# Norm gain applied in the turned copies, and other slots for down's first operands, in a two-layer encoder

## The chip, the core and the metric

The kernel runs on one core of a Trainium2 chip. The metric is the device time of one execution, in microseconds (us). The engines are TensorE (PE: matmuls; PEld is its weight load), VectorE (DVE), ScalarE (ACT), GpSimd (POOL) and SyncE (SP, which issues the DMAs). Each engine works through its own instructions in order and waits on semaphores for what others must finish first.

## The reference

Two encoder layers over 512 tokens of 1024 channels. Each layer is a feed-forward, a mixer of four attention groups and a second feed-forward, each followed by a residual sum and a norm:

```
def _layer_norm(x, g, b):
    mu = jnp.mean(x, -1, keepdims=True)
    xc = x - mu
    var = jnp.mean(xc * xc, -1, keepdims=True)
    return xc * lax.rsqrt(var + NORM_EPS) * g + b

def _swiglu(h, w_gu, w_down):
    gate, up = jnp.split(h @ w_gu, 2, axis=-1)
    return (jax.nn.silu(gate) * up) @ w_down

def reference(x, ...):
    alpha = (2 * DEPTH) ** 0.25
    for l in range(DEPTH):
        x = _layer_norm(alpha * x + 0.5 * _swiglu(x, ffn_w_gu[l, 0], ffn_w_down[l, 0]), ln_g[l, 0], ln_b[l, 0])
        mix = _token_mixers(x, w_in[l], ...)
        x = _layer_norm(alpha * x + mix, ln_g[l, 1], ln_b[l, 1])
        x = _layer_norm(alpha * x + 0.5 * _swiglu(x, ffn_w_gu[l, 1], ffn_w_down[l, 1]), ln_g[l, 2], ln_b[l, 2])
    return x
```

The feed-forward's hidden width is 2816.

## The kernel before

**Tiles.** The tokens lie in four tiles x0 to x3 of 128 tokens by 1024 channels. Every matmul operand is split into a high part (a cast, on ScalarE) and a low part (the rest, a subtraction on VectorE), and each product is made of three matmuls: high by high, high by low, low by high.

**The feed-forward** (`ffn`, L322) works through 11 pairs (`Pair`, L370); a pair is 256 columns of gate and of up. Each pair is a two-by-two block product, done with seven smaller products (`product`, L356) of 24 matmuls of 128x256 instead of eight. Their weights are sums of four loaded blocks (`prep_rest`, L392), their x operands are sums of blocks of the turned x, called al1 to al7. Products 1 and 2 go to banks ga and gb (`run12`), and `run_rest` (L420) goes on with 6 in ga, 5 in a new bank gc, then 7 in ga, 3 in gc and 4 in ga. Between 6 and 7 ScalarE copies ga out as u2 (L425), since the partial sum is needed by itself. The weights' high parts wh (L351) and low parts wl (L352) have rings of four buffers each: the cast of the fourth product after one waits until that one has been read.

**Down** (L472 to L511) then multiplies the 22 chunks of 128 hidden columns by w_down, into eight banks acc. A chunk's operands hh (cast, L480) and hl (subtraction, L481) are made from the stored h0 and h1 of its pair, into slots of two tags: even pairs into "v", odd ones into "p" (L476). The "v" slots also hold al3 (L160), which every pair reads.

**The norm** (`layer_norm`, L291) adds acc to x, takes statistics (bn_stats, bn_aggr), computes the factor on GpSimd (L303, L304), and then makes four VectorE operations of 128x512 a tile: subtract the mean and multiply by the gain (L307, two halves), multiply by the factor and add the offset (L314). Where a norm leads into a feed-forward, `to_al` (L186) turns the tile by eight TensorE transposes into two PSUM banks (xtp), copies them out and makes the splits: tiles 0 and 1 give al1 and al2 and the kept copies ac, tiles 2 and 3 give al4, 5, 7, 6 and 3, in this order. This happens four times: at the start of the program, from the mixer of each layer to its second feed-forward, and between the layers.

**What sets the order.** The program is written out in Python; a scheduler then orders each engine's instructions by program order and its own estimate of when they can start. So an instruction written later can stand earlier on its engine.

Of the kernel before, what the change touches and what calls it, by code (L numbers as in the profile page):

```python
# [11 lines left out]
F32 = mybir.dt.float32  # L12
# [60 lines left out]
def tile_encoder(ctx: ExitStack, tc: tile.TileContext, d: dict, out: bass.AP):  # L73
# [111 lines left out]

    def to_al(t):  # L186

        i = t % 2
        if t < 2:
            for g, b in turned_x(t):  # L190
                kept[g, i] = b4("hl", "ac")
                se.copy(kept[g, i], b)
                al_split(1 + g, i, b, -1.0)
            return
        (_, b0), (_, b1) = list(turned_x(t))
        a22 = b4("tb", "a22")
        se.copy(a22, b1)
        al_split(4, i, b1, -1.0)
        t5, t7 = b4("tb", "t5"), b4("tb", "t7")
        ve.tensor_tensor(t5, b0, a22, op=ALU.subtract)  # L200
# [90 lines left out]
    def layer_norm(t, accs, c, gb, shared=False):  # L291


        stt = sm.tile([P, 2, 6], F32, tag="bn", name="bn", bufs=2)
        xs = [x[t][:, n * FD:(n + 1) * FD] for n in range(2)]
        for n in range(2):
            ve.scalar_tensor_tensor(xs[n], accs[n], c * INV_A, xs[n], op0=ALU.mult, op1=ALU.add)
        for n in range(2):
            ve.bn_stats(stt[:, n], xs[n])
        mv = sm.tile([P, 2], F32, tag="mv", name="mv", bufs=2)  # L300
        ve.bn_aggr(mv, stt)  # L301
        rs = sm.tile([P, 2], F32, tag="rs", name="rs", bufs=2)
        ge.tensor_scalar(rs[:, 0:1], mv[:, 1:2], 1.0, EPS * INV_A * INV_A, op0=ALU.mult, op1=ALU.add)  # L303
        ge.tensor_tensor(rs[:, 1:2], rs[:, 0:1], mhalf[:, 0:1], op=ALU.pow)  # L304
        both = range(1 if shared else 2)
        for n in both:
            ve.scalar_tensor_tensor(xs[n], xs[n], mv[:, 0:1], gb[2 * n], op0=ALU.subtract, op1=ALU.mult)  # L307
        if shared:
            ge.tensor_scalar(rs[:, 0:1], mv[:, 0:1], rs[:, 1:2], -1.0, op0=ALU.mult, op1=ALU.mult)
            se.activation(xs[1], xs[1], AF.Identity, bias=rs[:, 0:1], scale=rs[:, 1:2])  # L310
            ge.tensor_tensor(xs[1], xs[1], gb[2], op=ALU.mult)
            ge.tensor_tensor(xs[1], xs[1], gb[3], op=ALU.add)
        for n in both:
            ve.scalar_tensor_tensor(xs[n], xs[n], rs[:, 1:2], gb[2 * n + 1], op0=ALU.mult, op1=ALU.add)  # L314


# [5 lines left out]
    def ffn(l, f, last, to_next):  # L322
# [47 lines left out]
        class Pair:  # L370
# [21 lines left out]
            def prep_rest(self):  # L392
                r = self.r
                add = lambda o, a, b: ve.tensor_tensor(o, a, b, op=ALU.add)  # L394
                add(r[11], r[11], r[12])
                t2 = raw_tile("t2")
                add(t2, r[11], r[22])
                self.w[6] = parts4(t2)
                self.w[5] = parts4(r[11])
                add(r[12], r[12], r[22])  # L400
                self.w[7] = parts4(r[12])
                self.w[3] = parts4(r[22])
                add(r[21], r[21], t2)
                self.w[4] = parts4(r[21])
                return self
# [14 lines left out]
            def run_rest(self):  # L420
                v3 = lambda t: t.rearrange("p (c t) -> p c t", c=2)
                a = self.a
                product(6, a, self.w[6], False)
                u2 = v3(tmp("u2"))
                se.copy(u2, a)  # L425
# [30 lines left out]
        p1.run12()  # L456
        gb = gain_tiles(l, 2 * f)
        if opening:
# [5 lines left out]
        for j in range(2, NB):  # L464
            p = Pair(j).load().prep12().prep_rest()
            p.run12()
            p.run_rest()
        acc = [[bank(tag, f"acc{t}{n}") for n, tag in enumerate(two)]
               for t, two in enumerate((("pt", "pt"), ("pv", "pj"), ("pj", "pj"), ("s", "s")))]
        hparts = {}  # L470

        def h_of(c, t):  # L472

            j = c // 2
            if j not in hparts:
                tag = ("v", "p")[j % 2] if c < NC - TAIL else "oT"  # L476
                hparts[j] = []
# [21 lines left out]
        if to_next:  # L499
            to_next[0]()  # L500
        for t in range(NT):
            for n in range(2):
                for i in range(TAIL):
                    down(t, NC - TAIL + i, ws[i], (n,))
            layer_norm(t, acc[t], 0.5, gb, last and t == NT - 2)
            if last:
# [155 lines left out]
    def mixer(l):  # L662
# [796 lines left out]
        def finish(t, accs):  # L1459
            layer_norm(t, accs, 1.0, lngb)  # L1460
            to_al(t)

# [17 lines left out]
    for l in range(DEPTH):  # L1480
        ffn(l, 0, False, (new_xT, to_xT))
        mixer(l)
        ffn(l, 1, l == DEPTH - 1, (new_al, to_al) if l < DEPTH - 1 else None)

# [21 lines left out]
```

## Time and profile before

| | us |
|---|---|
| median of 3 runs | 1984.5 (1984.44 to 1985.53) |
| profiled execution | 1989.4 |
| its span in the trace | 1987.6 |
| mean granted TensorE clock in it | 0.983 of full |
| start of the program, 0 to 50: PE busy | 36.48 of 50 |
| pairs of the first feed-forward, 50 to 250: PE, DVE, ACT busy | 198.07, 157.55, 101.14 of 200 |
| first down, 250 to 310: PE, DVE busy | 60.00, 24.84 of 60 |
| first mixer, 310 to 590: PE, DVE busy | 268.84, 206.42 of 280 |
| its transition into the next feed-forward, 632 to 680: PE, DVE busy | 34.76, 46.22 of 48 |

The span is cut by time: the start, then in each layer pairs, down, mixer, transition, pairs, down. In the profile's lines a group reads "line engine operation output<-input form", with the buffers' numbers left out; a bracket holds the idle time before an instruction and what released it. Matmuls are pipelined, so the distance from one start to the next is the time one takes, and the duration shown is longer.

### The profile page before, as it was taken

The numbers are of one execution on the slowest core, as the hardware profiler recorded it, in microseconds if no ns is written. First come the engines' busy times: TensorE is split into PE (matmuls) and PEld (weight loads), VectorE is DVE, ScalarE is ACT, GpSimd is POOL, SyncE is SP. The second block draws the span as 40 slices with busy tenths as digits, with TensorE's granted clock in tenths as the row PEclk, the third lists the DMA queues.
The fourth block names the chain that finished last, engine by engine and source line by source line (L and its number), as shares of the span: only waits on it lengthen the run. The fifth ranks groups of instructions, "written<-read, shape, count | busy, mean of one in ns | idle before, by whom it ended". The sixth has DMA issues, their size and how long they took to land.

```text
span 1987.6 us, 31884 instructions
## 1 busy us (share of the span) xinstructions
PE 1906.2 (96%) x12396; PEld 1735.7 (87%) x12396; DVE 1450.0 (73%) x2229; ACT 960.0 (48%) x1593; POOL 269.5 (14%) x411
## 2 busy tenths in 40 slices
PE   7999999999999899999999999999999979999998
PEld 6999988788887899988889999887887869999886
DVE  7887742858999978763598787337689998878535
ACT  5544532248774554443155545322587745444421
POOL 0000000335741000000000000004366300000001
PEclk9999999999999899999999999999999989999999
DMA  5323233343442333332223323331533424232321
GB/s 196 120 88 115 97 101 105 86 112 89 112 112 86 96 110 103 107 127 96 85 77 106 121 92 99 110 120 47 141 93 92 118 74 128 92 112 84 106 97 62
DMA packets 156487, 204.53 MB, mean 103 GB/s; under 512 B 14064, under 2 KB 122608, under 8 KB 156336
## 3 DMA queue, kind: packets, MB, share of 16 engines
q1 hardware_dynamic: 156336, 202.49, 33.7%
q8 instruction: 98, 1.61, 0.3%
q14 instruction: 53, 0.43, 0.1%
HBM read 177.42 MB, written 2.10 MB: 90 GB/s over the span
## 4 chain that ended last, share of the span: by engine, by line
PE 85%; DVE 8%; POOL 2%; ACT 2%; issue 2%; DMA 1%; SPq 0%; DVEq 0%; POOLq 0%; ACTq 0%
PE ga L249 25%; PE acc L249 23%; PE gc L249 13%; PE gb L249 6%; PE nat L249 5%; PE op L249 3%; PE sc L249 3%; PE pjt L249 2%; PE pv L249 2%; PE ptb L109 2%; DVE p L591 1%; PE xtp L109 1%; DVE al L178 1%; POOL wl L222 0%; DVE x L314 0%
## 5 line engine op out<-in xcount | busy, mean ns | idle before, releaser
L249 PE MATMUL ga<-al,wh 128*128 128x256 f32 x2752 | 392.5, 285 | 12.4 <-ACT wh L351 11.7
L351 ACT CAST wh<-b 128x1024 fp32r<-128x1024 f32 x256 | 267.7, 1049 | 280.2 <-issue 164.7
L352 DVE TENSOR_TENSOR wl<-b,wh 128x1024 fp32r<-128x1024 f32 x256 | 311.2, 1219 | 120.9 <-ACT wh L351 120.9
L249 PEld LDWEIGHTS ga<-al,wh 128*128 128x128 f32 x2752 | 360.2, 194 | 13.0 <-ACT wh L351 12.1
L222 DVE TENSOR_TENSOR wl<-wr,wh 128x1024 fp32r<-128x1024 f32 (+1 forms) x92 | 112.2, 1220 | 232.1 <-ACT wh L221 232.1
L249 PE MATMUL acc<-wh,hh 128*128 128x512 f32 x704 | 272.9, 390 | 6.7 <-ACT hh L480 6.7
L249 PE MATMUL acc<-wh,hl 128*128 128x512 f32 x704 | 276.6, 393 | 1.1 <-DVE hl L481 1.1
L249 PE MATMUL acc<-wl,hh 128*128 128x512 f32 x704 | 276.5, 393 | 0.2 <-DVE wl L222 0.2
L221 ACT CAST wh<-wr 128x1024 fp32r<-128x1024 f32 (+2 forms) x98 | 101.5, 1040 | 269.1 <-PE acc L249 226.0
L249 PE MATMUL ga<-al,wl 128*128 128x256 f32 x1376 | 224.3, 286 | 0.0
L303 POOL TENSOR_SCALAR rs<-mv 128x1 f32<-128x1 f32 x24 | 9.9, 412 | 1498.8 <-DVE mv L301 1498.7
L249 PE MATMUL gc<-al,wh 128*128 128x256 f32 x1408 | 201.1, 285 | 4.6 <-ACT al L177 4.3
L249 PEld LDWEIGHTS ga<-al,wl 128*128 128x128 f32 x1376 | 192.2, 194 | 0.6 <-DVE wl L352 0.3
L249 PEld LDWEIGHTS gc<-al,wh 128*128 128x128 f32 x1408 | 184.3, 194 | 5.2 <-ACT al L177 4.5
L249 PEld LDWEIGHTS acc<-wh,hh 128*128 128x128 f32 x704 | 132.1, 188 | 34.5 <-ACT hh L480 7.5
L249 PEld LDWEIGHTS acc<-wh,hl 128*128 128x128 f32 x704 | 133.3, 189 | 30.3 <-DVE hl L481 2.8
L249 PEld LDWEIGHTS acc<-wl,hh 128*128 128x128 f32 x704 | 133.1, 189 | 28.4 <-DVE wl L222 0.6
L249 PE MATMUL gc<-al,wl 128*128 128x256 f32 x704 | 113.6, 284 | 0.0
L394 DVE TENSOR_TENSOR b<-b,b 128x1024 f32<-128x1024 f32 x88 | 107.4, 1220 | 5.5 <-DMA b<-in_ffn_w_gu_dram 4.2
L249 PEld LDWEIGHTS gc<-al,wl 128*128 128x128 f32 x704 | 97.6, 193 | 0.0
L351 ACT CAST wh<-t 128x1024 fp32r<-128x1024 f32 x44 | 46.2, 1049 | 105.6 <-DVE t L394 105.6
L249 PE MATMUL gb<-al,wh 128*128 128x256 f32 x640 | 90.8, 285 | 0.0
(280 smaller groups left out, 3414.6 us busy)
## 6 DMA issues: line engine op xcount, KB each, us to landing
b<-in_ffn_w_gu_dram SPq DMA_DIRECT2D x176, 512.0 KB, 3.6
wr<-in_ffn_w_down_dram SPq DMA_DIRECT2D x88, 512.0 KB, 3.2
wr<-in_w_in_dram SPq DMA_DIRECT2D x30, 512.0 KB, 3.7
k<-ph SPq DMA_DIRECT2D x64, 128.0 KB, 2.4
wr<-in_w_out_dram SPq DMA_DIRECT2D x16, 512.0 KB, 3.6
qs<-ph SPq DMA_DIRECT2D x32, 128.0 KB, 2.4
ln_g<-in_ln_g_dram SPq DMA_DIRECT2D x12, 256.0 KB, 4.1
ln_b<-in_ln_b_dram SPq DMA_DIRECT2D x12, 256.0 KB, 4.7
```

The costliest lines, as they stand in the source:

```text
L109: te.transpose(o, a, ident)
L178: ve.tensor_tensor(l[:, :, cs], v, h[:, :, cs].bitcast(F32), op=ALU.subtract)
L221: se.copy(h[:, w], r[:, w])
L222: (lo or ve).tensor_tensor(l[:, q], r[:, q], h[:, q].bitcast(F32), op=ALU.subtract)
L249: te.matmul(o, a, b, start=start, stop=stop, **kw)
L303: ge.tensor_scalar(rs[:, 0:1], mv[:, 1:2], 1.0, EPS * INV_A * INV_A, op0=ALU.mult, op1=ALU.add)
L351: se.copy(h, r[:, q])
L352: ve.tensor_tensor(lo, r[:, q], h.bitcast(F32), op=ALU.subtract)
L394: add = lambda o, a, b: ve.tensor_tensor(o, a, b, op=ALU.add)
L591: ve.tensor_tensor_reduce(p, sb, nd, -h.slope, h.sink[0] if h.sink else 3.0e38, ALU.add, ALU.min, m)
```

## The change

The norms that lead into a feed-forward go through a new `norm_to_al`. It leaves gain and offset out of x: ScalarE normalises the tile with mean and factor alone (two activations of 128x512 with scale and bias, and GpSimd makes the bias in a third small operation). The turned copy gets gain and offset while ScalarE copies it out of PSUM, in `whole`: there a channel is a partition, so each of the eight blocks of 128x128 is one activation with a column of scale and a column of bias from `gt`, a small tile loaded from a new input `ln_t` that the host lays out. The splits then read the copy, not PSUM. x itself is needed with its gain only at the residual sum after down, so `gain_later` makes it up by four VectorE operations a tile, written after pairs 2 to 5. In `to_al` the splits of tiles 2 and 3 come in the order 5, 6, 7, 4, 3, also at the start of the program, where there is no gain. In the pairs product 5 now stands before product 6, and its weights are made first. The norm's gain tiles are loaded at pair 6 instead of at the start of the feed-forward. For down, the tags of the operands are swapped: even pairs into "p", odd ones into "v".

```diff
-    def to_al(t):
+    def to_al(t, gt=None):
+        def whole(g, b, tag, name):
+            o = b4(tag, name)
+            if gt is None:
+                se.copy(o, b)
+                return o, b
+            for k in range(4):
+                kk = 4 * g + k
+                se.activation(o[:, k], b[:, k], AF.Identity, bias=gt[:, 1, kk:kk + 1], scale=gt[:, 0, kk:kk + 1])
+            return o, o
...
-                kept[g, i] = b4("hl", "ac")
-                se.copy(kept[g, i], b)
+                kept[g, i], b = whole(g, b, "hl", "ac")
                 al_split(1 + g, i, b, -1.0)
...
-        a22 = b4("tb", "a22")
-        se.copy(a22, b1)
-        al_split(4, i, b1, -1.0)
+        a22, b1 = whole(*turned[1], "tb", "a22")
...
         ve.tensor_tensor(t5, b0, a22, op=ALU.subtract)
+        al_split(5, i, t5)
         ve.tensor_tensor(t7, b0, kept[0, i], op=ALU.subtract)
-        al_split(5, i, t5)
         t6 = kept[0, i]
         ve.tensor_tensor(t6, t6, t5, op=ALU.subtract)
+        al_split(6, i, t6)
         al_split(7, i, t7)
-        al_split(6, i, t6)
+        al_split(4, i, b1, -1.0)
...
+    def norm_to_al(t, accs, c, l, i, gb):
+
+        if t == 0:
+            gt = sm.tile([P, 2, 8], F32, tag="gt", name="gt", bufs=1)
+            load(gt, d["ln_t"][l, i])
+            gained[:] = [gt, gb]
...
+        rs, mv = norm_factors(stt)
+        ge.tensor_scalar(rs[:, 0:1], mv[:, 0:1], rs[:, 1:2], -1.0, op0=ALU.mult, op1=ALU.mult)
+        for n in range(2):
+            se.activation(xs[n], xs[n], AF.Identity, bias=rs[:, 0:1], scale=rs[:, 1:2])
+        to_al(t, gained[0])
+
+    def gain_later(t):
+        for n in range(2):
+            xs = x[t][:, n * FD:(n + 1) * FD]
+            ve.tensor_tensor(xs, xs, gained[1][2 * n], op=ALU.mult)
+            ve.tensor_tensor(xs, xs, gained[1][2 * n + 1], op=ALU.add)
...
                 add(r[11], r[11], r[12])
+                self.w[5] = parts4(r[11])
                 t2 = raw_tile("t2")
                 add(t2, r[11], r[22])
                 self.w[6] = parts4(t2)
-                self.w[5] = parts4(r[11])
...
-                product(6, a, self.w[6], False)
-                u2 = v3(tmp("u2"))
-                se.copy(u2, a)
                 c = self.bank("pj", "gc")
                 product(5, c, self.w[5], True)
                 p5 = v3(tmp("p5"))
                 se.copy(p5, c)
+                product(6, a, self.w[6], False)
+                u2 = v3(tmp("u2"))
+                se.copy(u2, a)
                 product(7, a, self.w[7], False)
...
-        gb = gain_tiles(l, 2 * f)
...
+            if gained and j < 6:
+                gain_later(j - 2)
+            if j == 6:
+                gained.clear()
+                gb = gain_tiles(l, 2 * f)
...
-                tag = ("v", "p")[j % 2] if c < NC - TAIL else "oT"
+                tag = ("p", "v")[j % 2] if c < NC - TAIL else "oT"
```

What the scheduler makes of it is shown at three places. The rows are an engine's instructions in order (line, operation, output<-input with the buffers' numbers, shape, and the engines waited for).

The first place is VectorE in the first transition, where the norm's third and fourth tiles meet the splits. Before, x3's statistics end at bn_6961, and its aggregate, gain and offset follow the splits of x2:

```order
L299 BN_STATS bn_6961<-x3_89 128x6 [waits DVE_49]
L200 TENSOR_TENSOR t5_6923<-xtp_6909,a22_6919 128x512 [waits Activation_49]
L181 SCALAR_TENSOR_TENSOR al4_6761<-xtp_6914,al4_6761 128x4x128 [waits PE_49,Activation_49]
...
L178 TENSOR_TENSOR al3_6774<-ac_6825,al3_6773 128x2x128 [waits Activation_49]
L301 BN_AGGR mv_6966<-bn_6961 128x2
L418 TENSOR_TENSOR s1_7054<-gb_7056,s1_7054 128x512 [waits PE_49]
L178 TENSOR_TENSOR al3_6776<-ac_6825,al3_6775 128x2x128 [waits Activation_49]
L307 SCALAR_TENSOR_TENSOR x3_89<-x3_89,mv_6966,ln_g_6753 128x512 [waits DVE_49]
L307 SCALAR_TENSOR_TENSOR x3_89<-x3_89,mv_6966,ln_g_6757 128x512
L314 SCALAR_TENSOR_TENSOR x3_89<-x3_89,rs_6968,ln_b_6755 128x512 [waits DVE_49,Pool_49]
L314 SCALAR_TENSOR_TENSOR x3_89<-x3_89,rs_6968,ln_b_6759 128x512 [waits DVE_49]
```

Now the same place reads so (mv_6984 is x3's aggregate, t5_6940 the first split of x2):

```order
L348 BN_STATS bn_6979<-x3_89 128x6 [waits DVE_49]
L439 TENSOR_TENSOR b21_7031<-b21_7031,t2_7176 128x1024
L330 BN_AGGR mv_6984<-bn_6979 128x2 [waits DVE_49,Pool_49]
L358 TENSOR_TENSOR x0_86<-x0_86,ln_g_6753 128x512
L397 TENSOR_TENSOR wl_7111<-b11_7106,wh_7110 128x1024 [waits DMAHW7_49,Activation_49]
L359 TENSOR_TENSOR x0_86<-x0_86,ln_b_6755 128x512 [waits DVE_49]
L358 TENSOR_TENSOR x0_86<-x0_86,ln_g_6757 128x512
L215 TENSOR_TENSOR t5_6940<-t7_6935,a22_6930 128x512 [waits Activation_49]
...
L178 TENSOR_TENSOR al3_6774<-ac_6829,al3_6773 128x2x128 [waits Activation_49]
L397 TENSOR_TENSOR wl_7115<-b21_7108,wh_7114 128x1024 [waits DMAHW6_49]
```

x3's aggregate and pair 0's last sum (b21) moved ahead of x2's splits, five rows of later gain moved in (three of x0's are shown), and wl_7115, the low weights of pair 1's product 2, stand behind the splits.

The second place is TensorE in a pair of the first feed-forward; 40 other pairs read alike (in three, six matmuls stand where ten do here). Before, product 6 (al6) is followed by all of product 5 (al5):

```order
L249 MATMUL ga_730<-al6_92,wl_709 128x256 x4
L249 MATMUL gc_809<-al5_91,wh_712 128x256 x8
L249 MATMUL gc_809<-al5_91,wl_713 128x256 [waits DVE_49]
L249 MATMUL gc_809<-al5_91,wl_713 128x256 x3
L249 MATMUL gc_809<-al5_91,wh_712 128x256 x8
L249 MATMUL gc_809<-al5_91,wl_713 128x256 x4
```

Now ten matmuls of product 3 (al3) follow it, and then product 7 (al7), which waits for ScalarE:

```order
L265 MATMUL ga_722<-al6_92,wl_705 128x256 x4
L265 MATMUL gc_775<-al3_102,wh_713 128x256 [waits Activation_49]
...
L265 MATMUL gc_775<-al3_105,wh_713 128x256
L265 MATMUL gc_775<-al3_102,wl_714 128x256 [waits DVE_49]
L265 MATMUL gc_775<-al3_102,wl_714 128x256
L265 MATMUL ga_722<-al7_93,wh_709 128x256 [waits Activation_49]
```

In the same pair ScalarE now reads as follows; before, u2's copy stood behind the cast for product 4, and p5's behind that for the next pair's product 1:

```order
L396 CAST wh_718<-b21_683 128x1024 [waits PE_49,Activation_49]
L471 COPY p5_800<-gc_775 128x512 [waits PE_49]
L396 CAST wh_917<-b11_909 128x1024 [waits DMAHW3_49,PE_49,Activation_49]
L474 COPY u2_826<-ga_722 128x512 [waits PE_49]
L396 CAST wh_921<-b21_911 128x1024 [waits DMAHW4_49,PE_49,Activation_49]
```

In this order wh_917 belongs to product 1 of the next pair and takes the buffer of product 6's weights; u2's copy stands behind it.

The third place is ScalarE around the first down. Before, the operands of chunk 0 (hh_2755) are cast behind the last pair's s2:

```order
L221 CAST wh_2857<-wr_2855 128x1024 [waits DMAHW5_49,DVE_49,PE_49]
L441 ACTIVATE s2_2737<-ga_2554 128x512 [waits DVE_49,PE_49]
L480 CAST hh_2755<-h0_520 128x512
L480 CAST hh_2759<-h1_524 128x512
L480 CAST hh_2891<-h0_911 128x512
```

Now they stand in the second pair, at row 51 of the engine instead of 172:

```order
L486 ACTIVATE s2_514<-ga_176 128x512 [waits DVE_49,PE_49]
L529 CAST hh_2755<-h0_512 128x512 [waits DVE_49]
L396 CAST wh_543<-b21_293 128x1024 [waits DVE_49,PE_49,Activation_49]
L471 COPY p5_572<-gc_547 128x512 [waits PE_49]
L529 CAST hh_2759<-h1_516 128x512 [waits DVE_49]
```

and behind the last s2 it is the second pair's operands that are cast first (hh_2823 and hh_2827, chunks 2 and 3):

```order
L486 ACTIVATE s2_2737<-ga_2554 128x512 [waits DVE_49,PE_49]
L529 CAST hh_2823<-h0_675 128x512
L529 CAST hh_2827<-h1_679 128x512
L529 CAST hh_2959<-h0_1131 128x512
L529 CAST hh_3403<-h0_2735 128x512 [waits DVE_49]
```

Chunk 0's operands moved from the end of the pairs to their beginning, and the second pair's took their place.

More of the change, by code (lines that the diff above doesn't have):

```diff
@@ L299, in layer_norm @@
             ve.bn_stats(stt[:, n], xs[n])
[L300 to L304, printed above, removed]
+        rs, mv = norm_factors(stt)
         both = range(1 if shared else 2)
@@ L314, in layer_norm, with norm_factors @@
             ve.scalar_tensor_tensor(xs[n], xs[n], rs[:, 1:2], gb[2 * n + 1], op0=ALU.mult, op1=ALU.add)
+    def norm_factors(stt):
+        mv = sm.tile([P, 2], F32, tag="mv", name="mv", bufs=2)
+        ve.bn_aggr(mv, stt)
+        rs = sm.tile([P, 2], F32, tag="rs", name="rs", bufs=2)
+        ge.tensor_scalar(rs[:, 0:1], mv[:, 1:2], 1.0, EPS * INV_A * INV_A, op0=ALU.mult, op1=ALU.add)
+        ge.tensor_tensor(rs[:, 1:2], rs[:, 0:1], mhalf[:, 0:1], op=ALU.pow)
+        return rs, mv
+    gained = []
+    def norm_to_al(t, accs, c, l, i, gb):
[3 more added lines that the diff above has]
+            gained[:] = [gt, gb]
+        stt = sm.tile([P, 2, 6], F32, tag="bn", name="bn", bufs=2)
+        xs = [x[t][:, n * FD:(n + 1) * FD] for n in range(2)]
+        for n in range(2):
+            ve.scalar_tensor_tensor(xs[n], accs[n], c * INV_A, xs[n], op0=ALU.mult, op1=ALU.add)
+            ve.bn_stats(stt[:, n], xs[n])
+        rs, mv = norm_factors(stt)
+        ge.tensor_scalar(rs[:, 0:1], mv[:, 0:1], rs[:, 1:2], -1.0, op0=ALU.mult, op1=ALU.mult)
[3 more added lines that the diff above has]
+    def gain_later(t):
+        for n in range(2):
+            xs = x[t][:, n * FD:(n + 1) * FD]
+            ve.tensor_tensor(xs, xs, gained[1][2 * n], op=ALU.mult)
+            ve.tensor_tensor(xs, xs, gained[1][2 * n + 1], op=ALU.add)
     TAIL = 4
@@ L499, in ffn @@
         if to_next:
-            to_next[0]()
+            (to_next[0] if len(to_next) > 1 else new_al)()
         for t in range(NT):
@@ L504, in ffn @@
                     down(t, NC - TAIL + i, ws[i], (n,))
+            if to_next and len(to_next) == 1:
+                to_next[0](t, acc[t], 0.5, l, 2 * f, gb)
+                continue
             layer_norm(t, acc[t], 0.5, gb, last and t == NT - 2)
@@ L1459, in finish @@
         def finish(t, accs):
-            layer_norm(t, accs, 1.0, lngb)
-            to_al(t)
+            norm_to_al(t, accs, 1.0, l, 1, lngb)
         for gns, ts in (("B", range(NA)), ("AB", range(NA, NT))):
@@ L1482, in tile_encoder @@
         mixer(l)
-        ffn(l, 1, l == DEPTH - 1, (new_al, to_al) if l < DEPTH - 1 else None)
+        ffn(l, 1, l == DEPTH - 1, (norm_to_al,) if l < DEPTH - 1 else None)
 _INS = ["x", "w_in", "win_sink", "mla_q_norm", "mla_w_uq", "mla_kv_norm", "mla_w_ukv", "ax_q_norm", "ax_k_norm",
@@ L1497 @@
     given.update(shape_constants())
+    rows = [given[n].reshape(DEPTH, 3, KD, P).transpose(0, 1, 3, 2) for n in ("ln_g", "ln_b")]
+    given["ln_t"] = np.ascontiguousarray(np.stack(rows, 3))
     for n, a in given.items():
```

9 lines of the change are left out of this document (7 added, 2 removed).

## The prediction

> **What bounds the kernel now.** I read the page first, for the busy shares and the chain of work that ended last. Then I read the list of TensorE's waits, and last the timeline at the places that it names.
>
> ```profile
> span 1987.6 us, 31884 instructions
> PE 1906.2 (96%) x12396; PEld 1735.7 (87%) x12396; DVE 1450.0 (73%) x2229; ACT 960.0 (48%) x1593; POOL 269.5 (14%) x411
> PE 85%; DVE 8%; POOL 2%; ACT 2%; issue 2%; DMA 1%; SPq 0%; DVEq 0%; POOLq 0%; ACTq 0%
> ```
>
> TensorE is busy for 96% of the span, and 85% of the chain is its own. An edit can therefore win only where TensorE waits or runs below full clock, and it loses wherever it makes a new wait. The waits (engine, tile and line, then who released it and the line; total us, times, longest) that the edits touch are these:
>
> ```profile
> PE xtp L109 <- DVE x L314: 21.4, 8, 6.5
> PE ga L249 <- ACT wh L351: 11.7, 2, 6.0
> PE acc L249 <- ACT hh L480: 6.7, 4, 1.7
> ```
>
> The next rows are windows: the stretch, its length, then busy time of PE, PEld, DVE, ACT and POOL, and the granted clock. The first two hold the transitions from a mixer to a feed-forward (I call them T1 and T3), the third the one from feed-forward to feed-forward (T2), the fourth one pair of the steady loop, the last the entry into a down projection.
>
> ```profile
> 590.00:680.00 90.00, 76.76 (x486) 69.24 (x485) 86.83 (x144) 46.16 (x84) 9.79 (x17) 0.92 0.28 86
> 1570.00:1662.00 92.00, 79.12 (x487) 71.63 (x486) 87.56 (x143) 46.05 (x83) 9.77 (x17) 0.91 0.27 85
> 1000.00:1035.00 35.00, 31.24 (x234) 30.16 (x233) 34.30 (x49) 18.40 (x29) 2.72 (x4) 0.90 0.26 76
> 1078.13:1098.29 20.16, 20.16 (x170) 20.16 (x169) 16.45 (x17) 10.44 (x14) 0.00 (x0) 1.00 0.34 105
> 245.50:252.80 7.30, 5.37 (x17) 3.88 (x16) 5.26 (x9) 5.18 (x8) 0.00 (x0) 0.77 0.47 153
> ```
>
> In T1 and T3 TensorE idles for about 13 us, and VectorE is busy for 96% of the time: there VectorE is the bound. In the steady pair TensorE never stops, and VectorE has 3.7 us to spare.
>
> **Down's first operands.** This term is the surest. Timeline of TensorE at the first entry (start, duration; the bracket is the idle time before it and its releaser):
>
> ```profile
> 245.01 0.64 PE L249 MATMUL ga<-al,wl 128*128 128x256 f32 x4
> 247.31 1.20 PE L249 MATMUL acc<-wh,hh 128*128 128x512 f32 x4 [1.66 <-ACT hh L480]
> 248.77 0.50 PE L249 MATMUL acc<-wh,hl 128*128 128x512 f32 x1 [0.27 <-DVE hl L481]
> ...
> 252.75 0.40 PE L249 MATMUL acc<-wl,hh 128*128 128x512 f32 x1
> 252.99 0.39 PE L249 MATMUL acc<-wh,hh 128*128 128x512 f32 x1
> 253.22 0.39 PE L249 MATMUL acc<-wh,hl 128*128 128x512 f32 x1
> ```
>
> The four matmuls at 245.01 (0.12 each) are issued by 245.49. Then 14 go out up to 252.75, in 5.44 us from the first; at full clock, 0.23 each as in the last rows, they would be out by 245.49 + 3.22 = 248.71. So an entry loses 4.04 us: 1.93 of idle time and 2.11 of slow clock behind it. In the new order (shown above) the casts and subtractions for chunk 0 stand in the second pair, some 200 us ahead, and the first accumulating matmul waits for nothing. Those of the next two chunks stay behind the last pair, but they are wanted 48 x 0.23 = 11.0 us in, and the same operations of before let matmuls go 2 and 3.5 us in. Four entries: **-16.2**. The bounds are -7.7, if only the idle time goes, and -16.2.
>
> By the Trainium skill ("TensorE: Matmul & The Clock Gate", "What's actually happening") the clock falls only after a whole idle window of about 3.4 us. By that rule these gaps would not slow the matmuls, and the edit would be worth its idle time alone. The trace disagrees: 1.66 us idle are followed by 14 matmuls in 5.44 us, at a granted clock of 0.77.
>
> **Product 7's wait (new).** Here the change loses. One steady pair, TensorE and then ScalarE:
>
> ```profile
> 1077.65 0.64 PE L249 MATMUL ga<-al,wl 128*128 128x256 f32 x4
> 1078.13 1.12 PE L249 MATMUL gc<-al,wh 128*128 128x256 f32 x8
> 1081.01 1.12 PE L249 MATMUL ga<-al,wh 128*128 128x256 f32 x8
> 1077.91 1.05 ACT L351 CAST wh<-b 128x1024 fp32r<-128x1024 f32 x1 [1.02 <-PE ga L249]
> 1078.86 0.58 ACT L425 COPY u<-ga 128x512 f32<-128x512 f32 x1
> ```
>
> Product 6 ends in bank ga; u2 is copied out behind a cast of 1.05 us that the same product released, and is done at 1079.44, or 1.31 us after TensorE went on. Product 7 writes the same bank. Before, the 24 matmuls of product 5 lie between (2.88 us, 0.12 each), and the copy has 1.57 us to spare. Now product 5 is ahead, and in 41 of 44 pairs ten matmuls of product 3 lie between: 1.20 us. ScalarE has the same pair of rows in the new order, since a cast again reuses product 6's slot. So product 7 misses the bank by 0.11, and I add 0.05 for the release. Starting again costs too:
>
> ```profile
> 633.15 0.38 PE L249 MATMUL ga<-al,we 128*128 128x256 f32 x1 [0.42 <-DVE bn L299]
> 633.37 0.28 PE L249 MATMUL ga<-al,wh 128*128 128x256 f32 x1
> 1021.52 1.10 PE L249 MATMUL ga<-al,wh 128*128 128x256 f32 x7 [0.68 <-DVE al L178]
> 1022.46 0.64 PE L249 MATMUL ga<-al,wl 128*128 128x256 f32 x4
> ```
>
> After 0.42 us idle the first matmul holds the next up by 0.22 instead of 0.12, so 0.10 more; after 0.68 the clock is still full. 0.26 x 41 = **+10.7**, with bounds of 0 (the copy comes in time) and +18 (0.45 a pair). Product 4 then waits for VectorE's sum of product 7, with 14 matmuls (1.68 us) between instead of 24; that sum takes 0.69, and I cost this at nothing while VectorE has its 3.7 us.
>
> **The transitions.** In T1 and T3 TensorE waits twice for long: at x3's transposes, and at product 6 of pair 0. The rows are of T3; T1 reads alike. Then VectorE in T1:
>
> ```profile
> 1628.96 1.94 PE L109 MATMUL xtp<-ident,x 128*128 128x128 f32 x8 [6.51 <-DVE x L314]
> 1642.31 2.08 PE L249 MATMUL ga<-al,wh 128*128 128x256 f32 x8 [5.67 <-ACT wh L351]
> 639.41 1.28 DVE L299 BATCH_NORM_STATS2 bn<-x 128x6 f32<-128x512 f32 x2
> 640.61 0.69 DVE L200 TENSOR_TENSOR t<-xtp,a 128x512 f32<-128x512 f32 x1
> 641.22 0.68 DVE L181 SCALAR_TENSOR_TENSOR al<-xtp,al 128x512 fp32r<-128x512 f32 x1
> 646.76 1.41 DVE L307 SCALAR_TENSOR_TENSOR x<-x,mv,ln_g 128x512 f32<-128x512 f32 x2
> 648.09 1.41 DVE L314 SCALAR_TENSOR_TENSOR x<-x,rs,ln_b 128x512 f32<-128x512 f32 x2
> ```
>
> x3's statistics are ready at 640.69, but x2's splits stand before its aggregate, and x3 comes out at 649.50. VectorE loses four such operations a tile, 2.8 us, 11.3 in four tiles. Of the later gain and offset, five operations (0.6 each, as the two splits at 640.61 and 641.22 follow each other) stand inside the transition: 3.0. So it has 8.3 us less there, and as it is the bound, that is the most that can be won. x3's aggregate now comes ahead of x2's splits, and pair 0's sums ahead of both, so both long waits go.
>
> ScalarE takes the work on. The nearest rows:
>
> ```profile
> L310 ACT ACTIVATE x<-x,rs 128x512 f32<-128x512 f32 x1 | 0.8, 813 | 21.1 <-POOL rs L309 21.1
> L192 ACT COPY ac<-xtp 128x512 f32<-128x512 f32 x16 | 9.4, 588 | 39.8 <-PE xtp L109 39.8
> L1139 ACT ACTIVATE bsq<-nat 128x128 f32<-128x128 f32 x8 | 2.5, 314 | 0.0
> L181 DVE SCALAR_TENSOR_TENSOR al<-xtp,al 128x256 fp32r<-128x256 f32 x32 | 12.8, 418 | 7.4 <-ACT al L180 7.4
> L309 POOL TENSOR_SCALAR rs<-mv,rs 128x1 f32<-128x1 f32 x1 | 0.8, 817 | 0.1
> ```
>
> A tile costs two of L310, and 8 activations of 128x128 with scale and offset. Each lies between 0.31 (L1139) and 0.54 (with the 0.23 by which L310 is above L192). I take 0.39 as spacing, 1.6 for a half instead of 0.59; with POOL's third operation the path from statistics to split halves is some 3 us longer.
>
> Setting the new order against these durations, I get in T1 0.9 us idle at the first transposes, 1.35 at product 1 (x1's low half), 3.0 at product 2 of pair 1 (its wl stands behind 15 rows of splits) and 1.3 at product 5, together 6.6 in place of 13.2. Two stretches of slow clock stay, as before. That makes -6.6, and -8.3 is the limit; I take **-7.5** for each, **-15.0** for both, bounds 0 and -8.3 each.
>
> T2 is another matter. Its waits for x were short, and there the scheduler puts ten gain operations (6.0 us) into the transition, the first ahead of x1's norm. My schedule has product 1 start 2.5 us later than before and product 5 wait 3.7 for its low half, and the shorter splits win part back: **+1.5**, bounds -5.3 (11.3 less 6.0) and +4.
>
> The opening has no gain, only the new order of splits: al4 comes last, so the bank for x3's second half comes free some two VectorE operations of 0.6 later: **+1.2**, bounds 0 (VectorE isn't late there) and +2.4 (four operations). Behind the transitions the gain costs 2.4 us in a pair where VectorE has 3.7 free: nothing, and at most 4 us if that cover is gone. The gain tiles are loaded later, where the DMA engines are under half busy, and the load of the turned gain adds one small transfer at each transition: nothing.
>
> **The sum.** -16.2 + 10.7 - 15.0 + 1.5 + 1.2 = -17.8. The profiled execution took 1989.4 (span 1987.6) and would take 1971.6; the median of the runs shown is 1984.5, which gives **1966.7**, rounded to 1966.5.
>
> **Rivals.**
> - *Product 7's wait outweighs all (slower).* The rest wins 28.5 us, so the wait decides from 28.5 / 41 = 0.70 us a pair. That needs u2's copy to stand behind one more cast: 1.05 more, 1.31 a pair, +53.7 - 28.5 = +25, about 2010. Against it: the order has one cast there, and the clock stays full after 0.68 us idle. The Trainium skill (same page, "A second HAM failure mode: psum-queue depth-cycling") tells of a clock that falls when TensorE idles briefly and often; 41 such falls at 2.11 would be this case too. 0.07.
> - *ScalarE becomes the bound of T1 and T3.* Four small activations in place of one copy sit on the path of every split; if they take 0.54 and VectorE waits for each, the 15.0 go: -2.8, or 1981.7. For it: VectorE already waits 7.4 us for ScalarE's casts in the row of L181. 0.13.
> - *The copy is in time.* A copy 0.16 us earlier, and the 10.7 go: 1956. 0.12.
> - *Down wins its idle time alone*: the slow clock at the four entries doesn't come from the gap, and stays. 8.5 less, 1975; the four gaps all have it behind them, which speaks against. 0.06.
>
> The forecast keeps 0.62.
>
> **Range and chances.** 1954 to 1981: from below the case of the copy in time to the case of ScalarE, leaving out the slow case, part of ScalarE's and the far ends of the transitions. About 0.2%, 4 us, is what a measurement of this kernel can tell from no change. Faster by more: nearly all of the forecast, of the copy in time and of down's case, and a third of ScalarE's: 0.84. Within: the rest of ScalarE's, 0.09. Slower: 0.07.
>
> **What would show it.** Right: no wait of acc for hh, and 0.23 us spacing at the four entries; some 41 waits of ga for u2 of 0.1 to 0.2 us; no wait of 5 us or more in T1 and T3, but 1 to 4 us at gb for wl and at gc for the splits; T2 about as long as before. Wrong: waits of ga for u2 above 0.5 us, half-clock stretches inside the pairs, waits at product 4 for VectorE's sum, or xtp waiting for ScalarE's x for more than 3 us.

## The result and the profile after

| | before | changed |
|---|---|---|
| median, us | 1985.0 (4 runs, 1984.4 to 1989.0) | 1970.2 (4 runs, 1968.4 to 1971.6) |
| ratio of the runs, 95% interval | | 0.9921 (0.9903 to 0.9938) |
| profiled execution, span, us | 1989.4, 1987.6 | 1970.0, 1968.2 |
| second profile (experiments below), span | 1984.7 | 1969.9 |

The change wins 14.8 us by the medians; the forecast was 1966.5, so 18 from the median that it started from. The range and the direction held. The page after, busy time by engine, and then the waits of TensorE that answer to those of before:

```profile
PE 1905.2 (97%) x12396; PEld 1727.2 (88%) x12396; DVE 1449.9 (74%) x2229; ACT 998.7 (51%) x1695; POOL 277.1 (14%) x423
PE xtp L109 <- DVE al L181: 6.3, 3, 3.4
PE xtp L109 <- ACT x L352: 6.3, 7, 1.4
PE gb L265 <- DVE wl L397: 5.8, 2, 2.9
PE gc L265 <- ACT al L177: 4.9, 3, 2.3
PE gc L265 <- DVE al L178: 2.3, 4, 1.1
PE ga L265 <- DVE al L181: 1.8, 2, 0.9
```

The two waits of over 5 us in T1 and T3 are gone, and so is every wait of acc for hh. In their place stand 2.9 us of gb for the low weights (twice) and some of 1 to 2 us for the splits. VectorE works as long as before, ScalarE 39 us longer.

The entry into the first down, and below it one pair of the steady loop (the matmuls, the weight load of product 7 and u2's copy):

```profile
249.77 0.64 PE L265 MATMUL ga<-al,wl 128*128 128x256 f32 x4
250.25 0.40 PE L265 MATMUL acc<-wh,hh 128*128 128x512 f32 x1
250.48 0.40 PE L265 MATMUL acc<-wh,hl 128*128 128x512 f32 x1
```

```profile
1072.34 1.12 PE L265 MATMUL gc<-al,wh 128*128 128x256 f32 x8
1073.30 0.40 PE L265 MATMUL gc<-al,wl 128*128 128x256 f32 x2
1073.69 1.22 PE L265 MATMUL ga<-al,wh 128*128 128x256 f32 x8
1074.75 0.64 PE L265 MATMUL ga<-al,wl 128*128 128x256 f32 x4
1073.69 1.01 PEld L265 LDWEIGHTS ga<-al,wh 128*128 128x128 f32 x8 [0.20 <-ACT u L474]
1073.06 0.58 ACT L474 COPY u<-ga 128x512 f32<-128x512 f32 x1
```

The entry has no gap: acc follows ga at full pace. In the pair u2's copy ends at 1073.64, product 7 starts at 1073.69 instead of 1073.54, and its first eight matmuls take 1.06 us instead of 0.96: 0.25 us, in every pair. The list of TensorE's waits does not hold this wait. The matmuls are pipelined, and the last two of product 3 still show as busy (0.40 us from 1073.30); it is the weight load that shows it, in the waits of PEld:

```profile
PEld ga L265 <- ACT u L474: 8.5, 44, 0.2
```

Two windows of the changed kernel: T2, which lies some 9 us earlier than in before, and one steady pair:

```profile
991.00:1026.00 35.00, 31.06 (x244) 29.81 (x244) 33.78 (x49) 27.30 (x49) 3.33 (x6) 1.00 0.29 91
1060.00:1080.40 20.40, 20.40 (x171) 20.20 (x170) 16.61 (x18) 10.44 (x13) 0.00 (x0) 1.00 0.32 104
```

In these 35 us TensorE is idle for as long as before (3.9 us, 3.8 in before's window), but at full clock (0.90 before). The new norm also makes it wait at two transposes ahead of the last acc: over the 50 us in which the whole transition lies, from 977 and in before from 988, it is idle for 6.0 us, before for 3.8. A pair takes 20.41 us from one copy of product 1 to the next, 20.16 before.

**Stages.** To set kernels beside each other, the span of each profile is cut at four kinds of marks: the start of ScalarE's copy of product 1 in pair 4 and in pair 10 of each feed-forward, the end of the last acc matmul, and the first matmul of the mixer's output (op). "Start" is from 0 to pair 4, a "down" from pair 10 to the last acc, T1 and T3 from the first op to pair 4, T2 from the last acc to pair 4. In start and T1 to T3 lie four of the waits for u2, so about 1.0 us where the kernel has them; pairs 4 to 10 are left out, since they differ by these waits alone. All in us, one profile each:

| kernel | start | down 1 | down 2 | down 3 | down 4 | T1 | T2 | T3 | median |
|---|---|---|---|---|---|---|---|---|---|
| before | 107.97 | 142.71 | 142.99 | 141.07 | 138.94 | 214.91 | 93.15 | 216.77 | 1985.0 |
| before_again | 109.02 | 141.09 | 141.37 | 142.57 | 140.53 | 215.52 | 93.31 | 215.08 | 1986.0 |
| changed | 111.00 | 138.75 | 141.55 | 138.77 | 136.72 | 209.66 | 91.56 | 207.43 | 1970.2 |
| changed_again | 112.39 | 138.91 | 141.70 | 138.80 | 136.67 | 209.71 | 91.59 | 207.08 | 1971.7 |
| slots_back | 112.65 | 141.39 | 144.11 | 141.26 | 139.16 | 207.65 | 94.08 | 209.55 | 1982.1 |
| slots_alone | 106.99 | 138.74 | 138.92 | 138.58 | 136.43 | 216.42 | 92.85 | 215.31 | 1972.7 |
| products_back | 110.20 | 138.61 | 141.45 | 138.53 | 136.43 | 210.12 | 91.19 | 210.23 | 1965.4 |
| first_pair_only | 110.13 | 138.62 | 141.39 | 138.66 | 136.46 | 206.82 | 92.36 | 209.00 | 1962.2 |
| norm_on_vector | 112.32 | 138.84 | 139.22 | 138.89 | 136.68 | 212.47 | 94.36 | 212.31 | 1979.3 |
| opening_back | 109.08 | 138.92 | 141.59 | 138.73 | 136.68 | 209.71 | 91.59 | 207.01 | 1969.8 |
| first_pair_and_opening | 108.58 | 138.48 | 141.37 | 138.56 | 136.46 | 208.04 | 92.33 | 208.95 | 1960.9 |
| first_opening_late_gains | 109.28 | 138.58 | 143.16 | 138.53 | 136.47 | 207.75 | 89.98 | 206.75 | 1959.3 |

(The median of before in the row of before_again is that of 15 runs beside the first four experiments.) Each down holds one wait for u2 as well, 0.25 us. Down 2 holds the first transposes of T2; where the norm is on ScalarE it is some 2.5 us longer, and that belongs to T2.

Two things make up most of the differences in T1 to T3: idle time (the stage less TensorE's busy time) and clock. The granted clock of these traces is 1.00 or 0.50, and apart from the program's end 0.50 comes in stretches of 3.41, 6.83 or 10.24 us. As time lost to it I count half of TensorE's busy time in such stretches. Idle time, then clock, in us:

| kernel | T1 | T2 | T3 |
|---|---|---|---|
| before | 16.5, 5.3 | 3.8, 2.9 | 16.1, 7.9 |
| before_again | 16.3, 5.8 | 3.7, 2.8 | 16.4, 5.7 |
| changed | 9.6, 5.8 | 3.9, 0 | 9.3, 3.0 |
| changed_again | 9.7, 5.8 | 4.0, 0 | 9.8, 1.7 |
| slots_back | 9.8, 2.8 | 3.7, 3.2 | 9.6, 5.7 |
| products_back | 11.4, 4.6 | 4.2, 0 | 11.5, 4.6 |
| first_pair_only | 9.5, 2.9 | 4.0, 1.7 | 9.6, 5.8 |
| norm_on_vector | 12.8, 4.7 | 4.2, 2.9 | 13.8, 3.2 |

The idle time is steady from one profile to the next of the same kernel, and between kernels that differ elsewhere; the clock is not.

### The profile page after: what moved, and what is told of

Read it like the earlier page. It is cut to its first block, busy times and chain, and to the rows that moved or that the text cites. A ratio compares the mean times of both kernels' runs of the same rounds, so it can differ in the third digit from the quotient of the medians.

```text
span 1968.2 us, 32043 instructions
## 1 busy us (share of the span) xinstructions
PE 1905.2 (97%) x12396; PEld 1727.2 (88%) x12396; DVE 1449.9 (74%) x2229; ACT 998.7 (51%) x1695; POOL 277.1 (14%) x423
## 4 chain that ended last, share of the span: by engine, by line
PE 84%; DVE 7%; POOL 3%; ACT 2%; issue 2%; DMA 1%; SPq 0%; DVEq 0%; POOLq 0%; ACTq 0%
PE ga L265 25%; PE acc L265 22%; PE gc L265 13%; PE gb L265 6%; PE nat L265 5%; PE op L265 2%; PE sc L265 2%; PE pjt L265 2%; PE pv L265 2%; PE ptb L109 2%; DVE p L643 1%; PE xtp L109 1%; DVE al L178 1%; DVE ptl L688 0%; POOL rs L333 0%
## 5 line engine op out<-in xcount | busy, mean ns | idle before, releaser
L265 PEld LDWEIGHTS ga<-al,wh 128*128 128x128 f32 x2752 | 354.4, 192 | 8.5 <-ACT u L474 8.5
L265 PE MATMUL gc<-al,wl 128*128 128x256 f32 x704 | 121.2, 286 | 0.0
L265 PEld LDWEIGHTS gc<-al,wl 128*128 128x128 f32 x704 | 101.8, 195 | 0.0
L685 ACT CAST pth<-ptb 128x512 fp32r<-128x512 f32 (+2 forms) x128 | 69.7, 545 | 41.4 <-PE ptb L109 40.1
```

Source lines behind the costliest of these rows:

```text
L265: te.matmul(o, a, b, start=start, stop=stop, **kw)
L685: se.copy(b.ph, b.tb[:, b.k0:b.k1])
```

## The experiments

Each is one edit of the changed kernel, unless it says otherwise. The runs of the kernel before beside them had medians of 1985.9 to 1986.5; the differences below are taken from the changed kernel's 1970.2, and 1971.7 in its second set of runs.

**before_again, changed_again.** No edit; a second profile of each kernel.

> The kernel before, unchanged, for a second profile. The two first profiles differ by 19.4 us in span (1987.6 and 1968.2), the medians by only 14.8. Theory A: the first profile of before was an execution with more slow clock than usual (1989.4 us against a median of 1984.5), and a second one has a span near 1983, with less lost behind the entries into down or behind the long waits of the transitions, at the same places. Theory B: the trace of before is typical and something outside the span makes the difference; then the span is near 1987 again.

Measured: span 1984.7, one run at 1986.5. The first mixer, from the last acc to the first op, took 149.59 us in the first profile of before and 146.48 in the second; in the twelve other profiles it took 146.1 to 147.7. So about 3 us of the first profile were not the kernel's usual time. There TensorE waits once for a DMA, and 3.41 us of half clock follow:

```profile
429.18 0.47 PE L249 MATMUL sc<-k,qs 128*128 128x512 f32 x1 [1.91 <-DMA k<-ph]
```

In before_again the same wait is 0.53 us and the clock stays full. Theory A holds for the sign, but the place is the mixer, which was not named. The entries into down also differ from one profile to the next; more on that below.

> The changed kernel, unchanged, for a second profile and a second median: all differences of the experiments are taken against its first, of four runs. Theory A (the terms are steady, and the spread of 2 to 3 us is slow clock behind short waits, here and there): median 1969 to 1971, and the transitions as in its first profile within 2 us each. Rival B (the first median was lucky or unlucky): outside 1968 to 1972, and the gains of all experiments shift by as much.

Measured: median 1971.7, 95% interval of the ratio 0.9912 to 0.9940; T1, T2 and T3 within 0.4 us of the first profile, the start 1.4 longer. Theory A. The differences below are uncertain by 1 to 2 us.

**slots_back.** The old slots for down's operands.

```diff
-                tag = ("p", "v")[j % 2] if c < NC - TAIL else "oT"
+                tag = ("v", "p")[j % 2] if c < NC - TAIL else "oT"
```

> The changed kernel with the old slots for down's first operands. Theory A (clock falls behind the gap, by an amount that depends on the entry): the four waits of acc for hh, 1.7 us each, come back, and the time is 8 to 16 us above the changed kernel, 1978 to 1986; from the two profiles (4.1, 4.0, 2.5 and 2.5 at the four entries) 13 us, 1983. Theory B (only the idle time is lost): 1.93 x 4 = 7.7 us, 1978.

Measured: 1982.1 (1979.4 to 1987.0), 11.9 above the changed kernel and 10.4 above its second median. The four waits are back (6.7 us for hh, 1.1 for hl), and the four downs are 2.5 us longer each. The time lies in theory A's range, but its cause, the clock, is not what costs here: the granted clock is 1.00 at all four entries. Theory B's idle time alone falls short, since an entry loses 2.5 us for 1.93 of shown idle time. The two times don't settle it to the microsecond: in this profile T1 loses 3.0 us less to the clock than in the changed kernel's, T2 and T3 some 3 more each.

**slots_alone.** The same swap, alone, in the kernel before.

> The kernel before with nothing changed but the slots for down's first operands. Theory A: all four waits of acc for hh go, and the time is 13 us below before (8 to 16), about 1972; the pairs stay at 20.16 us. Theory B (the casts, now early in the pairs, cost there what they win at the entry): within 4 us of before.

Measured: 1972.7, ratio 0.9934 (0.9920 to 0.9947), 13.4 us below the 1986.0 beside it. No wait of acc for hh is left, and the pairs stay at 20.16 us. Theory A: the swap wins 13 us wherever it stands, and costs nothing in the pairs. This is most of what the whole change wins.

What one gap costs is seen in three profiles with it, against 138.74, 138.92, 138.58 and 136.43 without: 4.0, 4.1, 2.5 and 2.5 us in before; 2.4, 2.5, 4.0 and 4.1 in before_again. In slots_back, beside the changed kernel, 2.6, 2.5, 2.5, 2.5. The third entry of before shows why:

```profile
1232.60 1.20 PE L249 MATMUL acc<-wh,hh 128*128 128x512 f32 x4 [1.66 <-ACT hh L480]
1234.06 0.50 PE L249 MATMUL acc<-wh,hl 128*128 128x512 f32 x1 [0.27 <-DVE hl L481]
1234.39 0.40 PE L249 MATMUL acc<-wl,hh 128*128 128x512 f32 x1
1234.62 0.39 PE L249 MATMUL acc<-wh,hl 128*128 128x512 f32 x1
```

The gap is the same 1.66 and 0.27, but from 1234.39 on the matmuls follow each other at 0.23, where the first entry stays slow until 252.75. The windows of the two entries (PE, PEld, DVE, ACT, POOL, granted clock) show the difference:

```profile
249.18:252.59 3.41, 3.41 (x10) 2.67 (x9) 2.83 (x6) 2.17 (x3) 0.00 (x0) 0.50 0.31 119
1232.00:1240.00 8.00, 7.14 (x30) 5.63 (x31) 5.37 (x12) 5.27 (x9) 0.00 (x0) 1.00 0.28 96
```

So an entry loses 2.5 us at full clock: the 1.93 us, and 0.5 more, because the first matmul after each of the two gaps holds the next up by 0.33 instead of 0.23 and some 0.16 us of each gap lie under the modelled end of the matmul before it. A stretch of half clock adds 1.6. Of the twelve entries four have it, the first two of before and the last two of before_again; the other eight have a granted clock of 1.00.

**products_back.** Product 6 before product 5 again, in every pair.

```diff
-                c = self.bank("pj", "gc")
-                product(5, c, self.w[5], True)
-                p5 = v3(tmp("p5"))
-                se.copy(p5, c)
                 product(6, a, self.w[6], False)
                 u2 = v3(tmp("u2"))
                 se.copy(u2, a)
+                c = self.bank("pj", "gc")
+                product(5, c, self.w[5], True)
+                p5 = v3(tmp("p5"))
+                se.copy(p5, c)
```

and the same for their weights in `prep_rest`.

> The changed kernel with product 6 before product 5 again in every pair. Theory A (product 7's wait costs 0.25 us in each pair and product 5 first is worth little elsewhere): the 44 waits of ga for u2 go, each pair takes 20.16 us instead of 20.41, and the time falls by 8 to 11 us, to 1960. Theory B (the order 5, 6 is what shortens the transitions): the pairs win 11 us, but the transitions wait for al6, one split more, and give back 3 us each, 9 in all: 1968 to 1970.

Measured: 1965.4, ratio 0.9896 (0.9883 to 0.9910), 4.8 below the changed kernel. The pairs are back at 20.16 us, so 44 x 0.25 = 11 us are won, and T1, T2 and T3 give some 6 of it back: against the changed kernel without its waits (1.0 less in each), T1 is 1.4, T2 0.6 and T3 4.0 us longer. By idle time it is 1.8 us in T1, 1.9 in T3 and 0.2 in T2; the other 2 us of T3 are clock (4.6 us against 3.0 and 1.7). Both theories are half right. Product 5 first is a loss over the whole kernel and a gain in the transitions.

**first_pair_only.** Product 5 first in the first pair of each feed-forward alone.

```diff
-                c = self.bank("pj", "gc")
-                product(5, c, self.w[5], True)
...
+                if self.j < 1:
+                    c, p5 = five()
                 product(6, a, self.w[6], False)
                 u2 = v3(tmp("u2"))
                 se.copy(u2, a)
+                if self.j >= 1:
+                    c, p5 = five()
```

(`five` holds the four lines on product 5 and its copy; the weights are ordered in the same way.)

> The changed kernel with product 5 before product 6 in the first pair of each feed-forward only; the other 40 pairs have the old order. Theory A (the order 5, 6 costs 0.25 us in each steady pair, and wins some 6 us at the transitions, all of it in the pair that follows the norm): 10 us below the changed kernel, 1960, and 5 below the one with the old order everywhere. Rival B (the 6 us that the old order gave back lie in the second pair too, or are chance): as fast as with the old order everywhere, 1965.

Measured: 1962.2, ratio 0.9880 (0.9867 to 0.9894), 8 below the changed kernel and 3 below products_back. Nearer to A: by idle time (9.5 and 9.6 us in T1 and T3, as in the changed kernel) all of what the order wins in the transitions lies in the first pair, and the steady pairs don't need it. The four first pairs keep their wait for u2.

**u2_on_vector.** The copy of u2 on VectorE, so that it no longer stands behind ScalarE's cast.

```diff
-                se.copy(u2, a)
+                ve.tensor_copy(u2, a)
```

> The changed kernel with u2 copied by VectorE instead of ScalarE, nothing else. Theory A (product 7 waits because the copy stands behind a cast of 1.05 us on ScalarE): the copy starts as product 6 ends, takes 0.7 us, and the wait goes; pairs of 20.16 us, and 10 us below the changed kernel, 1960. Rival B (VectorE, with 0.6 us more a pair, comes late with its sum after product 7): the wait moves to product 4, pairs stay above 20.3, 1968 or more.

Measured: 1965.1, ratio 0.9896 (0.9882 to 0.9909), 5 below the changed kernel. A pair now takes 0.07 to 0.08 us more than before instead of 0.25: the scheduler puts eight matmuls of product 3 between instead of ten, the copy (0.69 us) ends as they do, and a little of the restart is left. No wait moved to product 4. The cause of the wait is shown; the edit won about half of what was expected, 44 x 0.17 = 7.5 by the pairs. Its profile loses 1.7 us to the clock in T2 and 5.8 in T3, more than the changed kernel's.

**opening_back.** The old order of splits (4, 5, 7, 6, 3) at the start of the program alone.

```diff
+        if gt is None:
+            al_split(4, i, b1, -1.0)
         ve.tensor_tensor(t5, b0, a22, op=ALU.subtract)
```

(with the rest of the old order behind it.)

> The changed kernel with the old order of splits (4, 5, 7, 6, 3) at the start of the program only; products 5, 6 as changed. Theory A (al4 last holds a bank there and costs 2 us): 1 to 3 us below the changed kernel, 1968. Rival B (the start waits for al5 anyway, which the old order makes one split later): within 1 us of 1970.

Measured: 1969.8 with a wide spread (1964.4 to 1971.6), so the median alone says nothing. In the profile the start takes 109.08 us instead of 111.00 and 112.39, and no other stage of the table differs from both profiles by over 0.2. The place is the transposes of the last tile, which in the changed kernel wait for al4's split:

```profile
30.85 1.09 PE L109 MATMUL xtp<-ident,x 128*128 128x128 f32 x4 [3.38 <-DVE al L181]
```

With the old order this wait is gone, and product 5 waits 4.3 us for its split instead of 2.3. Theory A by the profile; by time it isn't shown.

**norm_on_vector.** The three norms by `layer_norm` on VectorE, gain and offset in x, no later gain. The copies are plain; the splits still read the copies.

```diff
     def norm_to_al(t, accs, c, l, i, gb):
+        layer_norm(t, accs, c, gb)
+        to_al(t, "plain")
```

> The changed kernel with the three norms back on VectorE, gain and offset in x before it is turned (layer_norm as before, no later gain); the copies are plain, but the splits still read them, and slots, products and the order of splits are as changed. Theory A (VectorE's 11.3 us less work in a transition is what T1 and T3 win): T1 and T3 each 6 to 8 us longer than in the changed kernel, T2 within 2, time 1982 to 1986, so hardly better than before plus the slots. Rival B (the order of splits and products does it, and ScalarE's part only moves work): within 4 us of the changed kernel, 1970 to 1974.

Measured: 1979.3, ratio 0.9969 (0.9956 to 0.9981), 9.1 above the changed kernel and 7.6 above its second median. T1 is 2.8 us longer, T3 5.0, T2 with its down 0.5. The waits of TensorE for x are back:

```profile
PE xtp L109 <- DVE x L326: 19.9, 8, 6.4
```

but the wait of ga for wh is not. Neither theory is right alone: of the 13.4 us of idle time that T1 and T3 win together, 7.4 come back here, and 6.0 stay won without the norm's move. The order of the products makes some 3.7 of these by products_back; what the order of sums and splits and the reading of the copies make of the rest was not tried one by one.

**gains_on_pool.** The later gain and offset on GpSimd.

```diff
-            ve.tensor_tensor(xs, xs, gained[1][2 * n], op=ALU.mult)
-            ve.tensor_tensor(xs, xs, gained[1][2 * n + 1], op=ALU.add)
+            ge.tensor_tensor(xs, xs, gained[1][2 * n], op=ALU.mult)
+            ge.tensor_tensor(xs, xs, gained[1][2 * n + 1], op=ALU.add)
```

> The changed kernel with the later gain and offset of x on GpSimd instead of VectorE. Theory A (VectorE bounds the transitions, and the gain operations that the scheduler puts there, 3.0 us in T1 and T3 and 6.0 in T2, cost about what they take): 2 us less at T1 and T3 each, 3 to 5 less at T2, 1962 to 1964. Rival B (they fill gaps of VectorE, or GpSimd's own rows for the next tile's norm now wait behind them, at 1.3 to 1.7 us each): within 3 us of the changed kernel, or slower.

Measured: 2010.4, ratio 1.0123 (1.0109 to 1.0136), 40 us above the changed kernel. Rival B, far beyond its size. GpSimd's timeline in T1, and below it TensorE's wait:

```profile
641.65 2.20 POOL L359 TENSOR_TENSOR x<-x,ln_b 128x512 f32<-128x512 f32 x1
643.80 1.71 POOL L358 TENSOR_TENSOR x<-x,ln_g 128x512 f32<-128x512 f32 x1
645.60 0.51 POOL L332 TENSOR_SCALAR rs<-mv 128x1 f32<-128x1 f32 x1
...
648.40 0.26 POOL L350 TENSOR_SCALAR rs<-mv,rs 128x1 f32<-128x1 f32 x1
PE xtp L109 <- ACT x L352: 30.3, 10, 7.5
```

Gain operations of 1.3 to 2.3 us each stand on GpSimd ahead of the next tile's three small norm operations, so the norm, the transposes and all behind them wait. Whether the gain rows on VectorE cost much in the changed kernel is left open by this run.

**first_pair_and_opening.** The edits of first_pair_only and opening_back together.

> Product 5 first in the first pair only, and the old order of splits at the start of the program: the two that were each tried alone. If the 2 us at the start that the profile of opening_back shows are real, 1 to 2 us below first_pair_only, 1960 to 1961. If they are chance, or the start needs al5 first when product 5 is first, 1962.

Measured: 1960.9, ratio 0.9872 (0.9857 to 0.9887); the start took 108.58 us against 110.13. It fits the 1 to 2 us of the profile, though the intervals of the two kernels overlap.

**first_opening_late_gains.** And the gain tiles for the later gain loaded after the second pair (their earlier loads go).

```diff
         p1.run_rest()
+        if gained:
+            gained[1] = gain_tiles(*gained[1])
```

> As first_pair_and_opening, and the gain tiles for x are loaded only after the second pair's instructions in the program, so that the scheduler takes the later gain for possible only later; in T2 its first row moves from behind x1's first sum to behind x2's statistics. Theory A (in T2 the gain rows ahead of x1's norm and the splits cost TensorE time): T2 2 to 4 us shorter, T1 and T3 0 to 2, 1955 to 1959. Rival B (the rows only move, or VectorE now stands waiting for the gain's DMA in front of the splits): as first_pair_and_opening within 2 us, or slower.

Measured: 1959.3, ratio 0.9867 (0.9853 to 0.9880), the fastest of all, but only 1.6 below the one before. T2 itself is 2.4 us shorter and the down ahead of it 1.8 longer. Of the 2.4, 1.7 are half clock that T2 has in the profile of first_pair_and_opening and not here. TensorE's idle time is 3.7 us in T2 and 2.9 in the down, against 3.9 and 2.2: a new wait for x of 2.8 us has come, while that at product 5 fell from 2.2 to 0.2. T3's 2.2 us are clock too (3.0 lost instead of 5.8). So moving the later gain rows won no idle time in T2, and theory A falls.

## Why the prediction was right, and where its sizes were off

The terms against the stages (mean of the two profiles of each kernel; the waits for u2 are taken off every stage and counted with product 7; down is taken against slots_alone, and what the second down is longer than there is counted with T2):

| term | predicted | measured |
|---|---|---|
| down's first operands | -16.2 | -13.1 (profiles), -13.4 (slots_alone), +10 to +12 when undone |
| product 7's wait | +10.7 | +11.0 (44 x 0.25) |
| T1 and T3 | -15.0 | -6.5 and -9.7 = -16.2 |
| T2 | +1.5 | -0.2 |
| start | +1.2 | +2.2 |
| sum | -17.8 | -16.3 |

**Down.** The mechanism was right; the term is too large by 3 us. The step that failed is "so an entry loses 4.04 us ... four entries": it took the slow clock of the first entry for all four. The third and fourth of the same profile have a granted clock of 1.00 and lose 2.5, and over three profiles eight entries of twelve do so. The rival that wins the idle time alone, 7.7, is refuted by slots_alone.

**Product 7.** 0.25 a pair against 0.26 predicted, with the same parts: copy ready at 1.30 after product 6, product 7 at 1.35 instead of 1.20, and 0.10 at the restart. The only miss is that the three pairs with six matmuls between have it too. The slow rival (0.70 a pair) didn't come: the clock stays at 1.00 in the pairs.

**T1 and T3.** The waits forecast for the new order came almost to the tenth in T1 (0.9 at product 1, forecast 1.35; 2.9 at product 2 of pair 1, forecast 3.0; 1.1 at product 5, forecast 1.3). In windows laid as the prediction's two were, TensorE is idle for 6.4 and 6.1 us, forecast 6.6, in place of 13.2 and 12.9:

```profile
588.00:678.00 90.00, 83.63 (x533) 75.09 (x532) 84.62 (x138) 62.65 (x123) 13.86 (x21) 0.94 0.30 93
1560.00:1652.00 92.00, 85.91 (x561) 77.18 (x560) 87.44 (x139) 62.90 (x122) 13.72 (x21) 0.96 0.32 99
```

Two steps failed beside that. "Two stretches of slow clock stay, as before" holds for the time lost in T1 (5.8 us, before 5.3 and 5.8), but T3 loses 3.0 and 1.7 us instead of 7.9 and 5.7, and that is why it wins more than T1, by idle time the same 6.7 us. That the sum of both still came near 15.0 is in part luck, since slots_back and first_pair_only have 5.7 and 5.8 in T3 again. And "VectorE has 8.3 us less there, and as it is the bound, that is the most that can be won" is not what limits it: norm_on_vector, with VectorE's norm operations all back, still has 6.0 us less idle time in T1 and T3 together than before. The order of the rows counts nearly as much as their number. ScalarE did not become the bound, and its prices were met:

```profile
L352 ACT ACTIVATE x<-x,rs 128x512 f32<-128x512 f32 x24 | 19.0, 827 | 30.7 <-DVE x L347 16.4 <-POOL rs L350 14.3
L199 ACT ACTIVATE ac<-xtp,gt 128x128 f32<-128x128 f32 x48 | 18.5, 476 | 0.1
L350 POOL TENSOR_SCALAR rs<-mv,rs 128x1 f32<-128x1 f32 x12 | 6.2, 513 | 1.2
```

0.48 us lies within the 0.31 to 0.54, and four take 1.5 us, as assumed (1.6).

**T2 and the start** are small. T2's waits at product 5 are 2.2 and 0.3 us, not 3.7. With its down it has 2.2 us more idle time, as a loss was forecast, and it comes out even only because it loses nothing to the clock, where before lost 2.9 and 2.8; the prediction didn't count on this. The start is 1 us worse than forecast. Its idle time grew by 1.6 us, and by opening_back's profile the order of splits is the cause.

**Cover.** The later gain cost nothing that is seen in the pairs: in T1's and T3's feed-forwards the profile shows no pair of over 21 us, and pairs 2 and 3 there took 19.6 and 20.9, so together 40.55 against 40.82 for two steady ones. In T2's feed-forward pair 2 took 20.9, 0.5 over a steady one.

Against the medians the sum is 1.5 us too large still (-16.3 and -14.8). The prediction's terms were taken from the first profile of before, whose mixer was some 3 us slower than in all others; but the mixer stands in no term, so this is not the 1.5. The mean spans of the two kernels' profiles are 17.1 us apart, the medians 14.8. Stretches of half clock, up to 1.7 us each, come and go between executions of one kernel, which would be enough; that they make this difference is not shown.

## What to carry to other kernels

A gap on TensorE in front of a long run of matmuls costs more than its length, here 2.5 or 4.0 us for 1.93 us of shown idle time, so operands that can be made early should be: here a swap of two slot tags alone won 13 of the 15 us. Before reordering products through a shared bank, count what stands between the product that is copied out and the one that overwrites it, against the copy and what the copying engine does first; 0.15 us short, in every pair, cost 11 us, and product 5 first in just the first pair kept its use. Before crediting an edit with what a stage won, split the stage into idle time and clock: T3's idle time fell by 6.7 us, as T1's did, and the further 3 us by which it beat T1 were clock. And an engine that computes the next tile's factor, however small the operation, is no place for bulk work that is due later.

## What the runs showed of the hardware that was not expected

The same gap of 1.93 us is followed by 3.41 us of half clock at some entries and by none at others, in the same kernel, and which entry it is changes between two profiles (entry costs of 4.0, 4.1, 2.5, 2.5 us in the first, 2.4, 2.5, 4.0, 4.1 in the second). In each of the three profiles with the gap, every change of the granted clock lies a whole multiple of 3.41 us from every other. Laid on that grid, the four entries with half clock have 1.59 to 1.93 us of the idle time in the one stretch just before it; in seven of the eight others the gap is split so that no stretch holds more than 1.55, and in the eighth one holds 1.66. So where the gap falls on the grid seems to decide, at about half a stretch; no run shifted a gap to test it.

The Trainium skill ("TensorE: Matmul & The Clock Gate", "What's actually happening") tells of a window that runs freely, so that the moment of a change of clock varies. The grid agrees with that. But by its length of idle time, about 3.4 us, no such gap should slow the clock at all, and here four of twelve did. Waits of 0.15 us, 44 of them, never lowered it: the granted clock is 1.00 over the steady pair above.
